# A hybrid encoder block on one core: a new opening, a new end of token mixing, and the gate column stored as single numbers from GpSimd's queue

## The chip, the cores and the metric

The kernel runs on one core of one Trainium2 chip. The metric is device time in microseconds (us). Three runs of the kernel before gave a median of 1852.78 us. One further execution was profiled; every duration below comes from that one.

## The reference, cut to what matters

One layer, one sequence of 256 frames, width 2048, all in float32:

```
mod = silu(c) @ w_ada + b_ada                     # nine vectors of 2048: shift, scale, gate, three times
x  += 1/2 * gt1 * rms(swiglu((rms(x) * (1 + sc1) + sh1) @ w_gu1) @ w_dn1)     # FFN 1, inner width 5504
h   = rms(x) * (1 + sc2) + sh2;  q, k, v, u, w = h @ w_in                     # token mixing
A   = chunked attention(q, k, v) + relative bias;   B = gelu(u) * (W_s norm(gelu(w)) + b)
x  += gt2 * rms(concat(rms(A), rms(B)) @ w_out)
x  += 1/2 * gt3 * rms(swiglu((rms(x) * (1 + sc3) + sh3) @ w_gu2) @ w_dn2)     # FFN 2
```

(The gains of the norms are left out of these lines.) Nothing of this is changed.

## The kernel before, in words

**Matrix products.** Every float32 weight tile is split in two float32r halves: ScalarE casts it (`hi`, L147), VectorE subtracts (`lo = raw - hi`, L148). A product is then three matmuls (L111 to L113): activations hi x weights hi, hi x lo, lo x hi. A weight tile (`raw`, 128 x 2048, 1 MB) arrives by one DMA on SyncE's (SP's) queue into one of three buffers and gives two split pairs of 128 x 1024. The pairs live in slots: four in the pool `wsp`, three more in a stage's own pool (`wx1`, `wx2`, `wx3`). A cast has to wait until the matmuls that read its slot before are done.

**The vectors `mod`.** `w_ada` is stored transposed. `ada_block` (L182) loads 128 rows of it (1 MB) and VectorE multiplies them by the broadcast row `c_bc` and sums along the row: one instruction of 128 x 2048 gives 128 numbers of one vector. There are 144 such blocks. 32 of them (scale and shift of FFN 1) are made in the opening, two for each of the 16 k-tiles (`kt`) of the activations; the other 112 are taken one by one from a list while weights are visited (`tick`), or all that are left of a vector at once (`flush_ada`).

**Opening (L533 to L562, and `first`).** x arrives in two tiles, then the row c as a broadcast of 1 MB, then two small tables. ScalarE squares both x tiles and applies silu to `c_bc`. VectorE scales x by 1/rms, TensorE transposes it, VectorE and ScalarE copy the transposes to `xnT`. `first(kt)` makes the two ada blocks of a k-tile, then `h` on ScalarE (L562), its cast `hhi` (L234) and its rest `hlo` on VectorE (L235). Matmuls on k-tile kt wait for these. To have work for TensorE while few k-tiles are ready, FFN 1 starts with a plan: a *visit* (c, p) takes chunk c of 512 columns and the k-tiles 2p and 2p+1, in 24 matmuls. The plan visits chunks 0, 4, 5, 3, 2, 1 with p = 0, then (1,1), (0,1), (1,2), (0,2), then (2,1) and so on. Chunk 0 keeps its PSUM banks, the others' sums are spilled to SBUF.

**End of token mixing (L866 to L900).** The product with `w_out` goes by two rows of frames (t = 0, 1) and column blocks of 512 (b). The part of B (`m_b`, names `mb`) is done in two pairs of column blocks, each over eight k-tiles and four weight tiles. A pair fills four PSUM banks out of six. When the first pair is done, `evac_b` adds each bank to `y` on VectorE (L867), ScalarE squares it for the norm, and VectorE multiplies by the row `gate` (L267). The second pair does t = 0 over all eight k-tiles, then t = 1. As soon as t = 0 is done, its norm, the addition to x (`post`, L278), the next norm and the transposes of `pre` (L247, `xtp`) lead to FFN 2.

**The gate row** (`gate`, L212 to L226) needs one vector of `mod` (128 partitions x 16 numbers, `gcol`) as a row on all partitions. TensorE transposes the column (`gps`), ScalarE copies it (`grow`), SP stores 16 rows of 512 B to DRAM (`gd`) and loads them back as a broadcast of 1 MB. It is made three times; the one for token mixing is `gate(1, ...)` at the end of mixing.

**Order.** The instructions of each engine stand in an order that a scheduler sets at build time; each engine and each DMA queue works in its order. `after(a, b)` forces a behind b on one engine.

Of the kernel before, what the change touches and what calls it, by code (L numbers as in the profile page):

```python
# [18 lines left out]
P = 128  # L19
# [24 lines left out]
class Lazy:  # L44
# [15 lines left out]
def block_kernel(ctx: ExitStack, tc: tile.TileContext, a: dict, out: bass.AP):  # L60
# [29 lines left out]

    x = load_x(a["x"])
    c_bc = const.tile([P, D], F32, tag="c_bc", name="c_bc")
    nc.sync.dma_start(c_bc, a["c"].partition_broadcast(P))
    vec = const.tile([P, V_N], F32, tag="vec", name="vec")
    nc.sync.dma_start(vec, a["vec"])
    bada = const.tile([P, 9 * KT], F32, tag="bada", name="bada")
    nc.sync.dma_start(bada, a["b_ada"])
# [29 lines left out]

    slots = {"seq": itertools.repeat(wsp), "hold": None}
# [15 lines left out]
    def split(raw):  # L144
# [3 lines left out]
        i_lo = nc.vector.tensor_tensor(lo[:, :n], raw, hi[:, :n].bitcast(F32), op=ALU.subtract)  # L148
        if order["split"]:
# [25 lines left out]
    def ada_block(m, kt, spare=None):  # L175
        if spare:
            st = yp.tile([P, D], F32, tag=spare, name=nm("ada"))
        else:
            st = adap.tile([P, D], F32, tag="ada", name=nm("ada"))
        i = m * KT + kt  # L180
        nc.sync.dma_start(st, a["w_ada"][i * P:(i + 1) * P, :])
        inst = nc.vector.tensor_tensor_reduce(  # L182
# [29 lines left out]
    def gate(i, factor, gp):  # L212
# [13 lines left out]
        nc.sync.dma_start(g, gd[:, :].rearrange("k p -> (k p)").partition_broadcast(P))  # L226
# [35 lines left out]
    def y_done(t, n, y, ysq, g, junk):  # L262

        ns = slice(n * CH, (n + 1) * CH)
        square(junk, y[t][:, ns], ysq[t], n, D)
# [22 lines left out]
    def ffn(wgu, wdn, h, avp, ahp, plan, rate, gate_of, finish, lead=(), after_lead=(), ahead=None):  # L288
# [169 lines left out]
        if plan:  # L458

            kts, credit = 0, 0.0  # L460
            held = plan[0][0]
            first(0)
            raw = gu_load(*plan[0])
            kts = 1
            for v, (c, p) in enumerate(plan):
                while kts < 2 * p + 2:
                    first(kts)
                    kts += 1
                fresh = c not in ps_of
                if fresh:  # L470
# [3 lines left out]
                rest = plan[v + 1:]  # L474
                nxt = [d for d, _ in rest if d != held]
                stop = c not in [d for d, _ in rest] or (c != held and nxt and nxt[0] != c)
                visit(c, p, fresh, bool(stop), bank_outer=v > 0, raw=raw)
                raw = None
                credit += 0.2
                while credit >= 1.0:  # L480
# [524 lines left out]
```

## Time and profile before

| What | us |
|---|---|
| runs, median of 3 | 1852.78 |
| the profiled execution | 1853.2 |
| its span, first to last instruction | 1851.4 |
| TensorE (PE) busy in the span | 1804.0 |
| VectorE (DVE) busy | 1334.6 |
| ScalarE (ACT) busy | 855.0 |
| GpSimd (POOL) busy | 27.6 |

The span leaves 1.8 us around it. PE counts as busy while a matmul is in flight, so time at half clock counts as busy too; the column PEclk of the stage view tells the two apart. In the timeline a row is: start, duration, engine, line, operation, output and input, count, and in brackets how long the engine had been idle and on what.

### The profile page before, as it was taken

The page shows a single profiled execution, that of the slowest core. Times are in us where ns is not written, and L with a number is a line of the kernel's source. Part 1 is how long each engine was busy: PE and PEld are TensorE (multiplying, and loading weights), DVE is VectorE, ACT ScalarE, POOL GpSimd, SP SyncE. Part 2 cuts the span into 40 slices and gives each one's busy share as a digit, 9 for nine tenths or more (in the row PEclk, how much of TensorE's full clock was granted, in tenths as well). Part 3 has the DMA queues.
Part 4 walks back from the last instruction along what each step waited for, and adds up shares of the span by engine and source line. Part 5 has one row for each costly group of instructions (what it writes and reads, how often), then busy time and mean ns, then how long its engine had stood idle before and what let it go on. Part 6 is the DMA issues. An engine that isn't in the chain of part 4 may idle for free.

```text
span 1851.4 us, 21252 instructions
## 1 busy us (share of the span) xinstructions
PE 1804.0 (97%) x8255; PEld 1499.9 (81%) x8255; DVE 1334.6 (72%) x1483; ACT 855.0 (46%) x1095; POOL 27.6 (1%) x54
## 2 busy tenths in 40 slices
PE   5999999999999999999999989999999999999997
PEld 4788888888888898788888867888888888888896
DVE  6888997998878776767889967777445555455455
ACT  5544455454344344745555447444444443443442
POOL 0000000000000000000001000000000000000000
PEclk8999999999999999999999999999999999999999
DMA  8888888889888876478788884887555555555462
GB/s 342 341 317 333 329 329 333 334 338 359 306 335 322 313 276 223 168 288 348 290 318 340 306 320 162 311 331 298 193 184 201 184 187 200 183 195 190 159 245 74
DMA packets 71478, 500.15 MB, mean 270 GB/s; under 512 B 8097, under 2 KB 8273, under 8 KB 12753
## 3 DMA queue, kind: packets, MB, share of 16 engines
q1 hardware_dynamic: 71376, 498.79, 71.2%
q8 instruction: 65, 1.06, 0.2%
q14 instruction: 37, 0.30, 0.0%
HBM read 494.54 MB, written 4.22 MB: 269 GB/s over the span
## 4 chain that ended last, share of the span: by engine, by line
PE 91%; DVE 4%; issue 2%; ACT 2%; DMA 1%; POOL 0%; POOLq 0%; DVEq 0%; ACTq 0%
PE gu L112 16%; PE gu L113 16%; PE gu L111 16%; PE dn L111 8%; PE dn L112 8%; PE dn L113 8%; PE pj L112 4%; PE pj L111 4%; PE pj L113 4%; DVE lo L148 1%; DVE ada L182 1%; PE atp L381 1%; PE wo L112 1%; PE wo L113 1%; PE wo L111 1%
## 5 line engine op out<-in xcount | busy, mean ns | idle before, releaser
L148 DVE TENSOR_TENSOR lo<-raw,hi 128x1024 fp32r<-128x1024 f32 (+1 forms) x628 | 752.0, 1209 | 418.9 <-ACT hi L147 417.5
L147 ACT CAST hi<-raw 128x1024 fp32r<-128x1024 f32 (+1 forms) x628 | 648.6, 1042 | 830.2 <-PE gu L113 453.0
L111 PE MATMUL gu<-hi,hhi 128*128 128x512 f32 (+1 forms) x1396 | 539.0, 387 | 14.8 <-ACT hi L147 7.5
L112 PE MATMUL gu<-lo,hhi 128*128 128x512 f32 (+1 forms) x1396 | 538.4, 386 | 0.1
L113 PE MATMUL gu<-hi,hlo 128*128 128x512 f32 (+1 forms) x1396 | 538.0, 386 | 0.0
L182 DVE CUSTOM_DVE_ANT_0 ada<-ada,c_bc,bada 128x2048 f32<-128x2048 f32 x144 | 337.5, 2345 | 14.6 <-DMA ada<-in_w_ada_dram 14.6
L111 PEld LDWEIGHTS gu<-hi,hhi 128*128 128x128 f32 x1396 | 263.3, 189 | 65.7 <-ACT hi L147 8.2
L112 PEld LDWEIGHTS gu<-lo,hhi 128*128 128x128 f32 x1396 | 263.2, 189 | 50.7 <-DVE lo L148 1.7
L113 PEld LDWEIGHTS gu<-hi,hlo 128*128 128x128 f32 x1396 | 263.2, 189 | 49.8 <-DVE hlo L235 0.2
L111 PE MATMUL dn<-hi,ah 128*128 128x512 f32 x640 | 249.1, 389 | 0.0
L113 PE MATMUL dn<-hi,al 128*128 128x512 f32 x640 | 249.0, 389 | 0.0
L112 PE MATMUL dn<-lo,ah 128*128 128x512 f32 x640 | 249.0, 389 | 0.0
L111 PEld LDWEIGHTS dn<-hi,ah 128*128 128x128 f32 x640 | 120.2, 188 | 25.1
L113 PEld LDWEIGHTS dn<-hi,al 128*128 128x128 f32 x640 | 120.2, 188 | 24.9
L112 PEld LDWEIGHTS dn<-lo,ah 128*128 128x128 f32 x640 | 120.2, 188 | 24.9
L112 PE MATMUL pj<-lo,hhi 128*128 128x512 f32 x304 | 120.9, 398 | 0.0
L111 PE MATMUL pj<-hi,hhi 128*128 128x512 f32 x304 | 120.8, 398 | 0.0
L113 PE MATMUL pj<-hi,hlo 128*128 128x512 f32 x304 | 119.9, 395 | 0.0
L111 PEld LDWEIGHTS pj<-hi,hhi 128*128 128x128 f32 x304 | 57.4, 189 | 11.0
L112 PEld LDWEIGHTS pj<-lo,hhi 128*128 128x128 f32 x304 | 57.3, 189 | 10.9 <-DVE lo L148 0.5
L113 PEld LDWEIGHTS pj<-hi,hlo 128*128 128x128 f32 x304 | 57.1, 188 | 10.9
L416 DVE TENSOR_TENSOR y<-y,dn 128x512 f32<-128x512 f32 x64 | 41.5, 681 | 4.6 <-PE dn L113 4.6
(159 smaller groups left out, 1064.5 us busy)
## 6 DMA issues: line engine op xcount, KB each, us to landing
raw<-in_w_gu_dram SPq DMA_DIRECT2D x160, 1024.0 KB, 4.8
ada<-in_w_ada_dram SPq DMA_DIRECT2D x144, 1024.0 KB, 6.9
raw<-in_w_dn_dram SPq DMA_DIRECT2D x86, 1024.0 KB, 4.8
raw<-in_w_in_dram SPq DMA_DIRECT2D x40, 1024.0 KB, 5.9
raw<-in_w_out_dram SPq DMA_DIRECT2D x16, 1024.0 KB, 7.8
raw<-in_w_gu_dram SPq DMA_DIRECT2D x16, 768.0 KB, 4.4
x<-in_x_dram SPq DMA_DIRECT2D x4, 1024.0 KB, 6.9
x<-x SPq DMA_DIRECT2D x4, 1024.0 KB, 4.7
```

The lines of the kernel that those rows point to most:

```text
L111: nc.tensor.matmul(ps, ah, wh, start=start, stop=False)
L112: nc.tensor.matmul(ps, ah, wl, start=False, stop=False)
L113: nc.tensor.matmul(ps, al, wh, start=False, stop=stop)
L147: i_hi = nc.scalar.copy(hi[:, :n], raw)
L148: i_lo = nc.vector.tensor_tensor(lo[:, :n], raw, hi[:, :n].bitcast(F32), op=ALU.subtract)
L182: inst = nc.vector.tensor_tensor_reduce(out=st, in0=st, in1=c_bc, scale=1.0, scalar=bada[:, i:i + 1], op0=ALU.mult, op1=ALU.add, accum_out ...
L381: nc.tensor.transpose(ps[:, q, :], av[:, q * P:(q + 1) * P], ident)
L416: nc.vector.tensor_tensor(y[t][:, ns], y[t][:, ns], ps[t], op=ALU.add)
```

## The change

1. **c and the tables.** c, `b_ada` and `vec` come as one table `small` (128 x 280) ahead of x. silu is applied to the 16 columns of c; TensorE spreads each over 128 columns (16 transposes of a broadcast column) and VectorE and ScalarE copy four banks to `c_bc`. The load of 1 MB and the silu over 128 x 2048 are gone.
2. **x.** VectorE squares half of the first x tile. The second tile is scaled on ScalarE; all eight copies to `xnT` are on ScalarE, three of them later.
3. **Loads.** The first two ada blocks are loaded right behind x; three more buffers (`early`) hold ada blocks until the plan ends.
4. **Plan.** The first two visits are cut in halves: k-tile 0 for chunks 0 and 4, then k-tile 1 for both, with weights loaded in halves. The order of this start is chained by hand on ScalarE and VectorE. After that each visit's splits are issued one visit ahead, and the ada blocks come one by one: 1.34 for each visit up to k-tile 5, then 0.7 (before: two at once, 0.4 for each visit).
5. **End of mixing.** The first pair of `m_b` runs with 1.5 ada blocks for each weight tile, and the gate row is made behind it in the program. Then two weight tiles of the second pair are split, and `evac_b` stands behind the last of these splits on both engines; x is loaded back after that.
6. **Gate row, all three times.** No transpose and no copy: `gcol` is stored as 2048 single numbers, and the broadcast load follows, both on GpSimd's queue.

```diff
+    small = const.tile([P, KT + 9 * KT + V_N], F32, tag="small", name="small")
+    nc.sync.dma_start(small, a["small"])
     x = load_x(a["x"])
-    nc.sync.dma_start(c_bc, a["c"].partition_broadcast(P))
...
-        ps = ptr.tile([KT, P], F32, tag="tr", name=nm("gps"))
-        nc.tensor.transpose(ps, col, ident)
-        row = sm.tile([KT, P], F32, tag="xn", name=nm("grow"), bufs=2)
-        nc.scalar.copy(row, ps)
         gd = dr.tile([KT, P], F32, tag=f"gd{i}", name=nm("gd"))
-        nc.sync.dma_start(gd, row)
+        with nc.allow_non_contiguous_dma(reason="2048 numbers"):
+            nc.gpsimd.dma_start(gd[:, :].rearrange("k p -> p k"), col)
         g = gp.tile([P, D], F32, tag="gate", name=nm("gate"))
-        nc.sync.dma_start(g, gd[:, :].rearrange("k p -> (k p)").partition_broadcast(P))
+        nc.gpsimd.dma_start(g, gd[:, :].rearrange("k p -> (k p)").partition_broadcast(P))
...
+            chain(first_act, hi0, h0[0], h0[1], late_evac[0], late_evac[1], late_evac[2], hi1, hi2, h1[0], h1[1], hi3)
+            chain(first_dve, *a0, *b0, lo0, h0[2], lo1, *a1, *b1, lo2, h1[2], lo3)
...
-                credit += 0.2
-                while credit >= 1.0:
-                    credit -= 1.0
-                    if kts < KT:
-                        first(kts)
-                        kts += 1
+                if v >= 3 and steps:
+                    credit += 1.34 if steps[0][0] < 6 else 0.7
+                    if steps[0][1] == 2:
+                        step()
+                    while steps and steps[0][1] < 2 and credit >= 1.0:
+                        credit -= step()
...
+    on_act.append(nc.scalar.activation(c_act, c_col, AF.Silu))
+    for j in range(4):
+        ps = pmm.tile([P, 4, P], F32, tag="mm", name=nm("cps"))
+        for q in range(4):
+            nc.tensor.transpose(ps[:, q, :], c_act[:, 4 * j + q:4 * j + q + 1].to_broadcast([P, P]), ident)
...
+        use_slots((wsp, 4), (wx2, 3))
+        tick_acc[1] = 1.5
+        ps = out_pair(m_b)
         flush_ada(GT[1])
         tick_acc[1] = 0.0
         gain(2, 0, KT)
         g = gate(1, 1.0, gp)
-        use_slots((wsp, 4), (wx2, 3))
-        ps = out_pair(m_b)
-        x2.extend(load_x(x_dram))
+        use_slots((adap, 1), once=((wsp, 3), (wx2, 3), (wsp, 1)))
+        sp = wo_visit() + wo_visit()
         for t in range(NT):
             for b in range(2):
-                evac_b(t, b, ps[b][t])
+                evac_b(t, b, ps[b][t], order["last"])
+        x2.extend(load_x(x_dram))
```

**How it moves instructions.** In the rows below ISA with the output `ada` is an ada block and ISA with the output `mod` reads out its sum.

VectorE in the opening, before, from the last part of x to the first split:

```order
L540 TENSOR_SCALAR xn_170<-x_2_89,r_154 128x512
L540 TENSOR_SCALAR xn_177<-x_2_89,r_154 128x512
L555 COPY xnT_185<-xtp_140 128x4x128
L555 COPY xnT_185<-xtp_147 128x4x128
L182 ISA ada_203,mod<-ada_203,c_bc,bada 128x2048
L182 ISA mod 128x1
L193 SCALAR_TENSOR_TENSOR gmul<-mod,vec 128x1
L182 ISA ada_206,mod<-ada_206,c_bc,bada 128x2048
L182 ISA mod 128x1
L235 TENSOR_TENSOR hlo_110<-h_33_210,hhi_109 128x256
L148 TENSOR_TENSOR lo_232<-raw_214,hi_231 128x1024
L148 TENSOR_TENSOR lo_236<-raw_214,hi_235 128x1024
```

and now:

```order
L643 TENSOR_SCALAR xn_174<-x_1_90,r_151 128x512
L643 TENSOR_SCALAR xn_181<-x_1_90,r_151 128x512
L176 TENSOR_REDUCE ms_156<-xsq_153 128x1
L202 ISA ada_114,mod<-ada_114,c_bc,small 128x2048
L202 ISA mod 128x1
L202 ISA ada_116,mod<-ada_116,c_bc,small 128x2048
L202 ISA mod 128x1
L214 SCALAR_TENSOR_TENSOR gmul<-mod,small 128x1
L156 TENSOR_TENSOR lo_240<-raw_226,hi_239 128x1024
L253 TENSOR_TENSOR hlo_113<-h_42_243,hhi_112 128x256
L156 TENSOR_TENSOR lo_248<-raw_228,hi_247 128x1024
L202 ISA ada_230,mod<-ada_230,c_bc,small 128x2048
```

The four scalings of the second x tile and all copies to `xnT` have left VectorE; one half tile of chunk 0 and one of chunk 4 are split before the blocks of k-tile 1.

VectorE at the end of mixing, before, from the last ada block of the gate to the first evacuations (`wo_82..` are the banks of the first pair):

```order
L182 ISA ada_8274,mod<-ada_8274,c_bc,bada 128x2048
L182 ISA mod 128x1
L215 SCALAR_TENSOR_TENSOR gcol_8278<-mod,vec 128x16
L148 TENSOR_TENSOR lo_8363<-raw_8360,hi_8362 128x1024
L148 TENSOR_TENSOR lo_8367<-raw_8360,hi_8366 128x1024
L148 TENSOR_TENSOR lo_8397<-raw_8394,hi_8396 128x1024
L148 TENSOR_TENSOR lo_8401<-raw_8394,hi_8400 128x1024
L867 SCALAR_TENSOR_TENSOR y_1527_7854<-wo_8288,r_8130,y_1527_7854 128x512
L867 SCALAR_TENSOR_TENSOR y_1527_7854<-wo_8290,r_8130,y_1527_7854 128x512
L867 SCALAR_TENSOR_TENSOR y_1528_7855<-wo_8289,r_8137,y_1528_7855 128x512
```

and now (the next row is the first product with `gate`):

```order
L236 SCALAR_TENSOR_TENSOR gcol_8445<-mod,small 128x16
L156 TENSOR_TENSOR lo_8413<-raw_8407,hi_8412 128x1024
L156 TENSOR_TENSOR lo_8417<-raw_8407,hi_8416 128x1024
L202 ISA ada_8409,mod<-ada_8409,c_bc,small 128x2048
L202 ISA mod 128x1
L156 TENSOR_TENSOR lo_8454<-raw_8451,hi_8453 128x1024
L156 TENSOR_TENSOR lo_8458<-raw_8451,hi_8457 128x1024
L156 TENSOR_TENSOR lo_8464<-raw_8461,hi_8463 128x1024
L156 TENSOR_TENSOR lo_8468<-raw_8461,hi_8467 128x1024
L968 SCALAR_TENSOR_TENSOR y_1528_7878<-wo_8286,r_8154,y_1528_7878 128x512
L968 SCALAR_TENSOR_TENSOR y_1528_7878<-wo_8288,r_8154,y_1528_7878 128x512
L968 SCALAR_TENSOR_TENSOR y_1529_7879<-wo_8287,r_8161,y_1529_7879 128x512
```

Four splits of the second pair and one ada block of the next vector now stand ahead of the evacuation.

TensorE in the second pair, before, where the last k-tiles of t = 0 (`wo_8448`, `wo_8450`) give way to t = 1 (`wo_8449`, `wo_8451`) on the first k-tile:

```order
L113 MATMUL wo_8448<-adas_8524,mb_7456 128x512
L111 MATMUL wo_8450<-adas_8524,mb_7455 128x512
L112 MATMUL wo_8450<-adas_8524,mb_7455 128x512
L113 MATMUL wo_8450<-adas_8524,mb_7456 128x512
L113 MATMUL wo_8449<-hi_8454,mb_7456 128x512
L111 MATMUL wo_8451<-hi_8454,mb_7455 128x512
```

and now, where t = 1 (`wo_8492`, `wo_8494`) begins behind the fourth k-tile of t = 0 (`wo_8491`, `wo_8493`, weights `hi_8467`):

```order
L114 MATMUL wo_8493<-lo_8468,mb_7479 128x512
L115 MATMUL wo_8493<-hi_8467,mb_7480 128x512
L113 MATMUL wo_8492<-hi_8453,mb_7479 128x512
L114 MATMUL wo_8492<-lo_8454,mb_7479 128x512
L115 MATMUL wo_8492<-hi_8453,mb_7480 128x512
L113 MATMUL wo_8494<-hi_8453,mb_7479 128x512
```

The first four k-tiles are now done for both t (48 matmuls) before the fifth k-tile of either; t = 0 is complete only 77 matmuls into the pair (before: 50).

More of the change, by code (lines that the diff above doesn't have):

```diff
@@ L126, in after, with chain @@
             mybir.DependencyClass.NoSync, mybir.DependencyReason.DATA), reason="order")
+    def chain(*insts):
+        for first, inst in zip(insts, insts[1:]):
+            after(inst, first)
+        return insts[-1]
     slots = {"seq": itertools.repeat(wsp), "hold": None}
@@ L260, in pre, with y_done @@
         order["ada"] = (inst[1], 2)
[L262 removed]
+    def y_done(t, n, y, ysq, g, junk, behind=None):
         ns = slice(n * CH, (n + 1) * CH)
[L265 removed]
+        inst = square(junk, y[t][:, ns], ysq[t], n, D)
+        if behind:
+            after(inst, behind[0])
         r = rstd(ysq[t]) if n == 3 else None
@@ L458, in ffn @@
         if plan:
-            kts, credit = 0, 0.0
             held = plan[0][0]
[L462 to L466, printed above, removed]
-                    first(kts)
-                    kts += 1
+            other = plan[1][0]
+            lead = [(c, p, (q,)) for q in range(2) for c, p in plan[:2]]
+            halves, late = {}, []
+            for c, p, (q,) in lead:
+                if c not in halves:
+                    halves[c] = wraw.tile([P, 2048], F32, tag="raw", name=nm("raw"))
+                off = 2 * D * CHUNKS[c][0] + p * P * 2048
+                nc.sync.dma_start(halves[c][:, q * 1024:(q + 1) * 1024],
+                                  wgu[off:off + P * 2048].rearrange("(p n) -> p n", p=P)[:, q * 1024:(q + 1) * 1024])
+                if (c, q) == (other, 0):
+                    late = [ada_load(m, 1) for m in (SC[0], SH[0])]
@@ new lines, in ffn, with half @@
+            plan = lead + [(c, p, (0, 1)) for c, p in plan[2:]]
+            ready_sp, dve, acts = {}, [first_dve], [first_act]
+            def half(c, q):
+                ready_sp[c, q] = {q: split(halves[c][:, q * 1024:(q + 1) * 1024])}
+                return order["last"]
+            a0, b0 = ada_first(0, 0, start_ada[0]), ada_first(0, 1, start_ada[1])
+            hi0, lo0 = half(held, 0)
+            h0 = h_first(0)
+            hi1, lo1 = half(other, 0)
+            a1, b1 = ada_first(1, 0, late[0]), ada_first(1, 1, late[1])
@@ L526, in ffn, with end_early @@
         down_last(C - 1, g)
-    h = new_h()
-    pts = []
-    xsq = [new_sums("xsq", 1) for _ in range(NT)]
-    for t in range(NT):
-        junk = yp.tile([P, D], F32, tag="y0", name=nm("junk"))
-        square(junk, x[t], xsq[t], 0, D)
-    nc.scalar.activation(c_bc, c_bc, AF.Silu)
+    wx = ExitStack()
+    wx1 = slots["hold"] = wx.enter_context(tc.tile_pool(name="wx1", bufs=3))
+    es = ExitStack()
+    early["pool"] = es.enter_context(tc.tile_pool(name="early", bufs=3))
+    def end_early():
+        if early["pool"] is not None:
+            early["pool"] = None
+            es.close()
@@ L561, in first, with ada_first, h_first @@
+    late_evac = [i_evac[1, j] for j in range(1, 4)]
+    first_dve = chain(*on_dve)
+    def ada_first(kt, i, st=None):
+        inst = ada_block((SC[0], SH[0])[i], kt, st)
+        return (inst, gain(0, kt, kt + 1)) if i else (inst,)
+    def h_first(kt):
         h32 = sm.tile([P, S], F32, tag="h32", name=nm("h32"), bufs=2)
-        nc.scalar.activation(h32, xnT[kt // 8][:, kt % 8, :], AF.Identity,
-                             bias=mod[:, SH[0] * KT + kt:SH[0] * KT + kt + 1], scale=gmul[:, kt:kt + 1])
```

161 lines of the change are left out of this document (103 added, 58 removed).

## The prediction

> **What bounds the kernel now.** I read the stage view first (stages chosen where the map of 40 slices shows PE below 9; columns: window, length, busy time of PE, PE's weight loads, DVE, ACT, POOL, granted clock, DMA share, GB/s).
>
> ```profile
> span 1851.4 us, 21252 instructions
> 0.00:23.00 23.00, 6.25 (x33) 5.11 (x33) 11.69 (x21) 11.58 (x15) 2.20 (x19) 0.94 0.93 377
> 23.00:52.00 29.00, 25.98 (x98) 20.48 (x99) 21.92 (x22) 17.38 (x25) 0.00 (x0) 0.87 0.76 303
> 52.00:100.00 48.00, 43.63 (x182) 34.60 (x181) 39.14 (x41) 23.52 (x33) 0.00 (x0) 0.96 0.86 339
> 100.00:720.00 620.00, 620.00 (x2822) 519.62 (x2821) 518.88 (x531) 271.73 (x301) 0.00 (x0) 1.00 0.84 322
> 1062.00:1079.00 17.00, 14.67 (x62) 10.58 (x60) 12.04 (x12) 7.89 (x11) 0.00 (x0) 1.00 0.83 322
> 1079.00:1110.00 31.00, 26.52 (x104) 20.91 (x105) 20.42 (x23) 14.85 (x24) 0.00 (x0) 0.89 0.85 335
> 1110.00:1150.00 40.00, 38.03 (x198) 31.68 (x197) 33.10 (x49) 31.32 (x65) 3.90 (x6) 1.00 0.43 158
> ```
>
> PE is the bound: from 100 to 720 it is never idle at full clock. Only its gaps can be won. The opening holds 24.1 us of them up to 100, plus stretches at a lower clock; the end of mixing holds 2.3 + 4.5 + 2.0 us between 1062 and 1150. The change touches both. What ends PE's waits there (us in total, times, longest):
>
> ```profile
> PE gu L111 <- ACT hhi L234: 7.2, 2, 4.3
> PE wo L111 <- ACT hi L147: 5.3, 3, 4.4
> ```
>
> **The opening.** The timeline shows the chain behind these waits.
>
> ```profile
> 8.12 1.91 ACT L162 ACTIVATE junk<-x 128x2048 f32<-128x2048 f32 x1 [0.55 <-DMA x<-in_x_dram]
> 16.03 2.34 DVE L182 CUSTOM_DVE_ANT_0 ada<-ada,c_bc,bada 128x2048 f32<-128x2048 f32 x1
> 20.94 0.60 ACT L562 ACTIVATE h<-xnT,mod,gmul 128x256 f32<-128x256 f32 x1 [4.72 <-DVE mod L182]
> 9.04 6.46 PE L546 MATMUL xtp<-ident,xn 128*128 128x128 f32 x32 [9.04 <-DVE xn L540]
> 22.98 0.80 PE L111 MATMUL gu<-hi,hhi 128*128 128x512 f32 x1 [7.47 <-ACT hi L147]
> 31.17 0.79 PE L111 MATMUL gu<-hi,hhi 128*128 128x512 f32 x1 [2.98 <-ACT hhi L234]
> 80.88 0.43 DVE L235 TENSOR_TENSOR hlo<-h,hhi 128x256 fp32r<-128x256 f32 x1 [1.10 <-ACT hhi L234]
> 80.89 0.50 PE L111 MATMUL gu<-hi,hhi 128*128 128x512 f32 x1 [4.25 <-ACT hhi L234]
> 83.67 0.63 PE L113 MATMUL gu<-hi,hlo 128*128 128x512 f32 x1
> 84.09 0.63 PE L111 MATMUL gu<-hi,hhi 128*128 128x512 f32 x1
> 92.83 0.40 PE L111 MATMUL gu<-hi,hhi 128*128 128x512 f32 x1
> 96.93 0.39 PE L111 MATMUL gu<-hi,hhi 128*128 128x512 f32 x1
> ```
>
> The first ada block starts at 16.03, because VectorE prepares x until then; k-tile 0 is ready at 22.98, k-tile 1 at 31.17, k-tile 5 only at 80.9. Then visit (2,1) ends at 97.2, and nothing waits after that. A matmul costs 0.228 us (18 starts from 92.83 to 96.93), and 0.43 us after a gap, while the clock is low.
>
> The costs of one instruction on VectorE and ScalarE, from the groups of the page (busy, mean ns), and small ones from the timeline:
>
> ```profile
> L148 DVE TENSOR_TENSOR lo<-raw,hi 128x1024 fp32r<-128x1024 f32 (+1 forms) x628 | 752.0, 1209 | 418.9 <-ACT hi L147 417.5
> L147 ACT CAST hi<-raw 128x1024 fp32r<-128x1024 f32 (+1 forms) x628 | 648.6, 1042 | 830.2 <-PE gu L113 453.0
> L182 DVE CUSTOM_DVE_ANT_0 ada<-ada,c_bc,bada 128x2048 f32<-128x2048 f32 x144 | 337.5, 2345 | 14.6 <-DMA ada<-in_w_ada_dram 14.6
> 13.87 1.07 ACT L553 COPY xnT<-xtp 128x512 f32<-128x512 f32 x2 [1.34 <-DVE xnT L555]
> ```
>
> *Start.* The x tiles still come as the first large loads, so the second square can follow its landing at 8.1. Ahead of it ScalarE now has silu of 16 columns, two copies of `c_bc` and half a square; the 16 transposes (before, 32 `xtp` with their waits took 6.5 us) can't start before `small` lands. No row shows `small`; a landing between 2.5 and 5 us bounds it by one x tile's 5, and I take 3.3. Copies then end near 7.6, the half square at 8.8, the second square at 10.9. VectorE's own part is done by then, so its first block starts near 12, not 16.03; two blocks of 2.42 with read-out, and the gain: 17.0, not 20.9. ScalarE has from 12.5 on four scalings and five copies (9 x 0.54 = 4.9), the cast 1.0, h 0.6, `hhi` 0.4: first matmul at 19.4, a lead of 3.6. The old load of c and its silu were not what came last.
>
> *To k-tile 5.* By the new order VectorE does from 12.0 on: 12 ada blocks (29.1), 18 splits (21.1 at 1.17), 6 `hlo` (2.6), 6 gains (1.0), together 53.8. Its waits in the new order: for the first cast behind the copies 1.4; for the second, behind the three late copies, 2.0; for the casts behind `hhi` 0.6; twice for slots that come free only at the end of a visit (1.5 and 1.3), 6.8 in all. Sum 72.6 for `hlo` of k-tile 5, against 81.3. Before, the same work took 65.3 from 16.03, so 11.5 us were waits and copies. At 72.6 PE is just short of work: visits 1 to 8 are 192 matmuls, from 19.4 some 44 us of matmuls with 5 us of low clock and gaps of 2 near k-tile 1, that is about 70; then 20 matmuls of (1,2) and two visits: 68 x 0.228 = 15.5, end of (2,1) at 88.1. **Gain 9.1 us.** Bounds: were VectorE never to wait, 16; were only the start to remain and `small` to land at 5, 2. The DMA cover is thinner than it looks (share 0.93 up to 23), but c's megabyte pays for the earlier ada loads. If the one-ahead splits didn't hide the ada blocks, every block in front of a split would cost 2.4.
>
> **The end of mixing.** Rows of the second place:
>
> ```profile
> 1055.73 2.35 DVE L182 CUSTOM_DVE_ANT_0 ada<-ada,c_bc,bada 128x2048 f32<-128x2048 f32 x1
> 1075.77 0.17 DVE L215 SCALAR_TENSOR_TENSOR gcol<-mod,vec 128x16 f32<-128x16 f32 x1
> 1078.48 0.32 SPq L226 DMA_DIRECT2D gate<-gd  x1
> 1087.25 2.11 DVE L867 SCALAR_TENSOR_TENSOR y<-wo,r,y 128x512 f32<-128x512 f32 x3 [4.99 <-PE wo L113]
> 1089.28 1.89 DVE L267 TENSOR_TENSOR y<-y,gate 128x512 f32<-128x512 f32 x3
> 1093.61 6.90 DVE L148 TENSOR_TENSOR lo<-raw,hi 128x1024 fp32r<-128x1024 f32 x6 [0.24 <-ACT hi L147]
> 1063.46 0.39 PE L111 MATMUL wo<-hi,mb 128*128 128x512 f32 x1
> 1088.79 0.39 PE L113 MATMUL wo<-hi,mb 128*128 128x512 f32 x1
> 1093.63 1.22 PE L111 MATMUL wo<-hi,mb 128*128 128x512 f32 x2 [4.45 <-ACT hi L147]
> 1107.38 1.43 DVE L867 SCALAR_TENSOR_TENSOR y<-wo,r,y 128x512 f32<-128x512 f32 x2 [3.12 <-PE wo L113]
> 1118.65 2.05 PE L247 MATMUL xtp<-dg,x 128*128 128x128 f32 x16 [0.88 <-DVE dg L243]
> ```
>
> *First pair.* 96 matmuls need 21.9 us, so from 1063.46 it could end at 1085.3; it ended at 1089.0. The new order spreads the ada blocks, and I find no wait left: 3.7 us earlier. *Restart.* The second pair needs a bank that `evac_b` frees, and that now stands behind every split. From 1055.73: 12 splits 14.0, 6 blocks 14.5, `gcol` 0.2, and waits of about 4 (for a cast behind ScalarE's four scalings of y, and for weight tiles queued on SP behind ada loads whose buffer is not yet free): 1088.4, plus one evacuation 0.7: PE restarts at 1089.1, before at 1093.63. 4.5 us ahead.
>
> *Given back.* t = 0 is complete after 77 matmuls, not 50. Before, from 1093.63 to 1107.4 was 13.8 for 50 (11.4 and 2.4 of low clock); now 17.5 + 2.4 after 1089.1 is 1109.0. The chain from there (evacuation, gate, norm, x, square, norm) took 11.3 to the first `xtp`; with two evacuations of t = 1 now inside it in place of a split, 11.5. So `xtp` starts at 1120.5 against 1118.65, with 3 matmuls fewer behind it (0.7). PE waits there some 7 us, not 0.9: the lead is lost to this stall. **Loss 1.2**, and 1.3 more for packets of the new stores between the weight loads (bounded by 0 and the 8 us below): 2.5. The bounds are -3 (if t = 0 isn't the last) and +10.
>
> *The gate row.* Its rows (DMA issues, KB each, us to landing; the queue's packets, MB, share):
>
> ```profile
> gate<-gd SPq DMA_DIRECT2D x1, 1024.0 KB, 7.9
> gd<-grow SPq DMA_DIRECT2D x1, 8.0 KB, 1.7
> q1 hardware_dynamic: 71376, 498.79, 71.2%
> ```
>
> Before, `gcol` at 1075.77 led to a landing at 1078.48 + 7.9 = 1086.4, ahead of its use at 1089.28. Now `gcol` comes at 1077.5. From the start of the gate products to the next finished split took 5.5 us (1089.28 to 1093.61 + 1.2), and the order gives PE 48 matmuls that need none of it: until 1089.1 + 10.9 + 2.4 = 1102.4. So the row must land by 1096.9; with 1 us of issue and 7.9 for the broadcast, the store has 10.5 us. No row shows 2048 packets of 4 B. From below, 16 packets took 1.7. From above, each of the 128 packets of an engine waits its turn behind a mean packet of the weights (0.712 x 16 x 1851.4 / 71376 = 0.296 us): 37.8. Ends so far apart are split by their geometric mean, 8: hidden, by 2.5 us. GpSimd waits in its queue between store and load; behind that stands only the norm of t = 0, which comes later. The transpose and copy taken off PE and ACT save 0.5 us of cover. The other two gate rows are made long before use.
>
> **Sum.** 1853.2 (the profiled execution, 0.4 above the median) - 9.1 + 2.5 = **1846.6 us**.
>
> **Rivals.**
> *A, the gate row comes late (slower).* Every microsecond of the store over 10.5 holds VectorE at the first gate product, with the splits of the fifth k-tile behind it, and PE runs dry. At 37.8 the row lands at 1077.5 + 1 + 37.8 + 7.9 = 1124.2, PE stalls 1124.2 - 1096.9 = 27.3: 1873.9, slower than before. It outweighs the gain from a store of 17 us on. For it: the DMA share of 0.85 there, and a share that the queue of weights always fills. Against: PE's stall stops the weight loads, and then the store runs free. Chance 0.2.
> [...]
> *B, the opening is no better.* ScalarE's part per visit in the first round is two casts, four spill copies and h, near 5.2 (2.0 + 4 x 0.54 + 1.0) of the 5.5 us of 24 matmuls; if casts come late by 1 us a visit, the 6.8 of waits become 14 and k-tile 5 arrives at 80: 1853.2 - 2 + 2.5 = 1853.7. Against: ACT is busy for 17.4 of 29 us there now. Chance 0.15.
> *C, both places gain.* A store as cheap as 1.7 and no traffic cost, and an opening with half the waits: 1853.2 - 12.5 - 2 = 1838.7. For it: 24 us of gaps; against: the longer way to t = 0. Chance 0.15.
> The forecast has 0.5.
>
> **How the numbers follow.** The forecast's own range is 1841 to 1852. C lowers the range to 1838, A with a store between 10 and 25 us raises it to 1861: 1838 to 1861 leaves out the far part of A and a little of C. A difference of 2% is about what a measurement of this kernel can tell from no change; it is 37 us, and no case but the far end of A with a further loss reaches it: faster 0.02, same 0.96, slower 0.02.
>
> **What would show it.** First `gu` matmul near 19.4; `hlo` of k-tile 5 near 72.6, (2,1) done near 88. If PE waits more than 5 us between 30 and 88, B. In mixing the first pair ends about 22 us after its start, the restart comes about 4 us later, and PE's longest wait there is in front of `xtp` behind `dg`. If instead the wait stands in front of `hi` or `lo` of the fifth k-tile with VectorE waiting for `gate`, A. The sum is wrong if (2,1) ends within 3 us of 97, or `xtp` comes more than 5 us off.

## The result and the profile after

The changed kernel takes 1865.78 us (median of 4 runs, 1863.36 to 1867.05), the kernel before 1853.28 beside it (median of 4). The ratio is 1.0067, with a 95% interval of 1.0047 to 1.0087: 0.7% slower. One of the four executions of the kernel before took 2025.89 us, and the ratio leaves it out. The profiled execution of the changed kernel has a span of 1862.8 us, 11.4 more than before.

The stage view of the changed kernel, in the stages of the prediction:

```profile
span 1862.8 us, 21298 instructions
0.00:23.00 23.00, 11.91 (x50) 9.93 (x50) 10.75 (x17) 13.54 (x23) 4.22 (x19) 1.00 0.92 363
23.00:52.00 29.00, 26.92 (x106) 21.55 (x105) 25.04 (x26) 18.27 (x28) 0.00 (x0) 0.94 0.84 351
52.00:100.00 48.00, 46.96 (x205) 37.59 (x204) 42.77 (x48) 26.14 (x35) 0.00 (x0) 1.00 0.97 390
100.00:720.00 620.00, 613.30 (x2772) 510.93 (x2771) 509.08 (x520) 266.04 (x294) 1.91 (x2) 1.00 0.82 313
1062.00:1079.00 17.00, 17.00 (x77) 14.08 (x76) 14.82 (x14) 7.68 (x9) 0.00 (x0) 1.00 0.85 335
1079.00:1110.00 31.00, 23.95 (x95) 17.96 (x93) 16.45 (x18) 8.30 (x13) 1.77 (x2) 0.94 1.00 288
1110.00:1150.00 40.00, 31.80 (x158) 27.05 (x159) 34.86 (x52) 33.20 (x69) 4.75 (x6) 0.91 0.51 189
```

Up to 100 us PE's gaps have shrunk: it is busy for 85.8 us there, not 75.9. But between 100 and 720, where before nothing waited, PE now stands still for 6.7 us, and between 1079 and 1150 for 15.2, not 6.5.

A table of stages with fixed bounds doesn't tell where the time went once everything has shifted. So I also numbered PE's wide matmuls (128x512, and 128x384 for the last chunk of `gu`) of the outputs `gu`, `dn`, `pj` and `wo` in the order of their starts (7632 in either trace) and compared the start of the k-th one. Minus is a lead over the kernel before:

| k | start before, us | place | changed kernel, us |
|---|---|---|---|
| 0 | 22.98 | first `gu` | -0.6 |
| 264 | 96.93 | end of visit (2,1) | -7.7 |
| 700 | 195.76 | first round | -4.3 |
| 1000 | 265.87 | end of the first round | -1.5 |
| 1400 | 358.36 | ahead of the hole at the first gate (below) | -1.5 |
| 1600 | 404.59 | behind it | +4.0 |
| 4300 | 1064.37 | first pair of `m_b` | +4.1 |
| 4400 | 1097.62 | second pair, just restarted | +0.2 |
| 4500 | 1126.94 | behind the `xtp` of t = 0 | +11.9 |
| 7000 | 1704.90 | second FFN | +11.4 |

Four things happened. The opening won 7.7 us; the first round took 6.2 of it back; 5.5 were lost near the first gate, a place to which the prediction gave nothing; and at the end of mixing 3.9 were won and 11.7 lost. The third gate (near 1285) cost nothing.

What ended PE's waits in the changed kernel:

```profile
PE wo L113 <- ACT hi L155: 8.0, 3, 4.7
PE xtp L265 <- DVE dg L261: 6.5, 1, 6.5
PE gu L113 <- ACT hhi L252: 4.2, 2, 2.2
PE gu L113 <- DVE acc L376: 4.2, 6, 1.1
PE dn L114 <- DVE lo L156: 1.8, 1, 1.8
```

`acc` is the spill of the first round: those six waits lie between 90 and 245 us. The wait in `dn` begins at 371.7, behind the first gate; behind it PE's granted clock is 0.51 from 373.8 to 377.3, where before it is 1.00.

The DMA view from 350 to 370 us, first of the changed kernel (GB/s in slices of 0.5 us; the other rows are the queue, the number of issues, KB each and the median us from issue to landing):

```profile
GB/s 426 426 426 328 393 311 410 492 229 229 344 344 410 377 393 344 377 378 334 319 100 0 49 82 82 66 66 49 66 82 33 66 33 49 66 33 131 66 393 410
ada<-in_w_ada_dram SPq DMA_DIRECT2D x2, 1024.0 KB, 16.3
raw<-in_w_gu_dram SPq DMA_DIRECT2D x2, 1024.0 KB, 13.6
gd<-gcol POOLq DMA_DIRECT2D x1, 8.0 KB, 13.3
```

and of the kernel before, which makes no transfer for the gate there:

```profile
GB/s 442 410 410 311 377 311 377 377 180 213 98 213 442 311 442 360 410 492 344 442 344 279 147 295 459 426 360 492 393 410 475 393 410 262 311 360 442 344 229 33
```

The store is issued at 353.5 and lands 13.3 us later; from 360 to 369 (18 slices) the whole core's transfers fall to some 60 GB/s. Weights under way then take 14 to 16 us from issue to landing; over the program their medians are 4.8 and 6.9. A second hole, of some 80 GB/s for 10 us, stands at the end of mixing; in the changed kernel from 1080 to 1100:

```profile
GB/s 377 361 229 246 360 360 360 279 377 393 410 459 393 414 301 233 49 33 99 49 33 83 246 49 180 147 164 66 33 49 33 33 16 49 82 131 197 393 377 410
q1 hardware_dynamic: 587, 4.27, 98.8%
x<-x SPq DMA_DIRECT2D x2, 1024.0 KB, 24.3
raw<-in_w_out_dram SPq DMA_DIRECT2D x2, 1024.0 KB, 20.2
gate<-gd POOLq DMA_DIRECT2D x1, 1024.0 KB, 10.3
gd<-gcol POOLq DMA_DIRECT2D x1, 8.0 KB, 14.0
```

Two weight tiles of `w_out` landed after 20 us, and VectorE shows what that did (timeline of the changed kernel):

```profile
1081.32 0.17 DVE L236 SCALAR_TENSOR_TENSOR gcol<-mod,small 128x16 f32<-128x16 f32 x1
1094.11 2.36 DVE L156 TENSOR_TENSOR lo<-raw,hi 128x1024 fp32r<-128x1024 f32 x2 [6.37 <-ACT hi L155]
1100.35 2.36 DVE L156 TENSOR_TENSOR lo<-raw,hi 128x1024 fp32r<-128x1024 f32 x2 [3.88 <-ACT hi L155]
1102.63 2.06 DVE L968 SCALAR_TENSOR_TENSOR y<-wo,r,y 128x512 f32<-128x512 f32 x3
1107.13 1.90 DVE L287 TENSOR_TENSOR y<-y,gate 128x512 f32<-128x512 f32 x3 [2.44 <-DMA gate<-gd]
```

The wait for the gate row itself is only 2.4 us. Ten more were already lost in front of the splits, behind casts whose weights came late. ScalarE's waits between 1062 and 1145 say whose they were:

```profile
ACT hi L155 <- DMA raw<-in_w_out_dram: 23.0, 4, 9.5
```

Before, the same group in this place was 5.6 us.

### The profile page after: what moved, and what is told of

Its sections match the earlier page's. It is cut to its first block, busy times and chain, and to the rows that moved or that the text cites. A ratio compares the mean times of both kernels' runs of the same rounds, so it can differ in the third digit from the quotient of the medians.

```text
span 1862.8 us, 21298 instructions
## 1 busy us (share of the span) xinstructions
PE 1810.7 (97%) x8268; PEld 1503.7 (81%) x8268; DVE 1331.7 (71%) x1479; ACT 856.4 (46%) x1102; POOL 36.5 (2%) x60
## 5 line engine op out<-in xcount | busy, mean ns | idle before, releaser
L202 DVE CUSTOM_DVE_ANT_0 ada<-ada,c_bc,small 128x2048 f32<-128x2048 f32 x144 | 337.3, 2344 | 24.2 <-DMA ada<-in_w_ada_dram 15.3
L178 POOL TENSOR_TENSOR r<-ms,mhalf 128x1 f32<-128x1 f32 x16 | 21.8, 1361 | 1033.5 <-DVE ms L176 1033.5
```

The costliest lines, as they stand in the source:

```text
L178: nc.gpsimd.tensor_tensor(r, ms, mhalf, op=ALU.pow)
L202: inst = nc.vector.tensor_tensor_reduce(out=st, in0=st, in1=c_bc, scale=1.0, scalar=bada[:, i:i + 1], op0=ALU.mult, op1=ALU.add, accum_out ...
```

## The experiments

Theory T1 was that the 2048 pieces of 4 bytes starve the weights wherever they are stored. T2 put it down to GpSimd's queue, T3 to the rebuilt order, with a store that costs nothing. Each run below changes the changed kernel, unless it says otherwise; "lead" is that of the table above, against the same trace of before. "Span" is that of the one profiled execution. Executions of one kernel differ by up to 6 us, so a difference of 1 or 2 us between two spans says little by itself.

**1. The old gate path back in the changed kernel.**

```diff
+        ps = ptr.tile([KT, P], F32, tag="tr", name=nm("gps"))
+        nc.tensor.transpose(ps, col, ident)
+        row = sm.tile([KT, P], F32, tag="xn", name=nm("grow"), bufs=2)
+        nc.scalar.copy(row, ps)
...
-        with nc.allow_non_contiguous_dma(reason="2048 numbers"):
-            nc.gpsimd.dma_start(gd[:, :].rearrange("k p -> p k"), col)
+        nc.sync.dma_start(gd, row)
...
-        nc.gpsimd.dma_start(g, gd[:, :].rearrange("k p -> (k p)").partition_broadcast(P))
+        nc.sync.dma_start(g, gd[:, :].rearrange("k p -> (k p)").partition_broadcast(P))
```

> The change with the gate path of before at all three places: transpose on TensorE, copy on ScalarE, store of 16 rows of 512 B and broadcast load on SyncE's queue. Theory T1 (the store of 2048 single numbers keeps the DMA engines from the weights for about 9 us wherever it stands): the lag against before stays at -1.5 us through the first gate (in the changed kernel it goes there from -1.5 to +4.0), and at the end of mixing ScalarE's waits for w_out weights fall from 23 us to under 10; span 1848 to 1852 (the changed kernel 1862.8). T3 (the new order at the end of mixing and the lead spent between 95 and 240 us are all of it, the store costs nothing): span within 3 us of 1862.8.

Span 1851.1, median 1851.85; ratio to before 0.9995 (0.9985 to 1.0005). The lead is 9.5 at k = 264 and 3.4 at k = 1000, and stays at 3.5 from k = 1400 to 1600; ScalarE's waits for `w_out` are 9.3 us. T1 holds and T3 falls. But the kernel is no faster than before either: with the store gone, the rest of the change shows no gain as a whole. A caveat: the transpose is put in PE's order at 687 us, so the first gate's transfers also stand elsewhere now; run 5 closes that.

**2. Rows of 512 B, but on GpSimd's queue** (`nc.gpsimd` in place of `nc.sync` for the store and the load of run 1).

> As the run with the row gate, but store (16 rows of 512 B) and broadcast load are issued by GpSimd. T1 (packet size): store lands in under 5 us, span within 2 us of the run with the row gate on SyncE's queue. T2 (it is GpSimd's queue, not the size of the packets): store and load still take 10 us or more each, span 1858 or more.

Span 1850.3 (one execution), store 3.7 us in the median. T2 falls: with rows the queue alone costs nothing (run 1 has 1851.1).

**3. Single numbers, but on ScalarE's queue** (`nc.scalar.dma_start(gd...)`).

> The change with only the store of 2048 single numbers moved from GpSimd's queue to ScalarE's; the broadcast load stays on GpSimd's. T1: the store still takes 9 us or more and the weights' rate falls under 100 GB/s for that time; span 1858 or more. T2: store in under 5 us, span 1848 to 1853.

```profile
gd<-gcol ACTq DMA_DIRECT2D x3, 8.0 KB, 17.9
q10 hardware_dynamic: 6192, 0.02, 0.2%
```

Span 1867.3 (one execution), at least as slow as from GpSimd. Here the trace counts each piece: 6192 packets are three times 2064. T2 falls again, but T1 holds in part only. At the first gate the rate does fall under 100 GB/s, for some 5 us, and 5.2 us of lead go. At the end of mixing it does not. The store is issued at 1079.6 and takes 24.9 us; these are the rates from 1080 to 1120 (slices of 1 us) and PE's wait there:

```profile
GB/s 311 410 418 426 402 393 434 426 443 402 393 418 443 434 410 377 402 451 369 183 42 9 0 0 0 0 213 393 401 41 0 8 0 0 0 0 0 0 139 385
PE wo L113 <- ACT hi L155: 15.2, 1, 15.2
```

Up to 1098 the transfers run at 311 to 451 GB/s beside the store. Here the row itself is late: VectorE waits 16.2 us for it, with the fifth k-tile's splits behind. So the same 2048 pieces cost time in two ways, and which one prevails differs with the queue and the place.

**4. Only the new gate path, in the kernel before.**

> The kernel before with only the gate path of the change (2048 single numbers and the broadcast load on GpSimd's queue). T1: lag of 3 to 6 us at the first gate (near 375 to 400 us), and 5 to 12 us more at the end of mixing, where the gate row would land 14 + 1 + 10 us behind its column (1075.8), near 1101, against its use at 1089: span 1860 to 1870 (before 1851.4). T3: within 3 us of 1851.4.

Span 1865.5, in the shortest of four executions; median 1871.22, ratio 1.0101 (1.0084 to 1.0118). The lag is +6.2 behind the first gate and +14.3 behind mixing. At the end of mixing VectorE shows

```profile
DVE y L264 <- DMA gate<-gd: 12.7, 1, 12.7
```

so in the old order, which has nothing to do meanwhile, the row itself is waited for. The span lies inside T1's range; the price at the first gate is just over its 3 to 6 us, that in mixing (8.1) inside.

**5. The column as it lies in SBUF: 128 pieces of 64 B, same queue, same place.**

```diff
-        gd = dr.tile([KT, P], F32, tag=f"gd{i}", name=nm("gd"))
-        with nc.allow_non_contiguous_dma(reason="2048 numbers"):
-            nc.gpsimd.dma_start(gd[:, :].rearrange("k p -> p k"), col)
+        gd = dr.tile([P, KT], F32, tag=f"gd{i}", name=nm("gd"))
+        nc.gpsimd.dma_start(gd, col)
...
-        nc.gpsimd.dma_start(g, gd[:, :].rearrange("k p -> (k p)").partition_broadcast(P))
+        nc.gpsimd.dma_start(g, gd[:, :].rearrange("p k -> (p k)").partition_broadcast(P))
```

> The change with the gate column stored as it lies in SBUF, 128 pieces of 64 B that follow one another in DRAM, on GpSimd's queue; the broadcast load reads the 8 KB as before, so the gate values come in another order than the reference's: the output is not the reference's, only the time counts. Theory N (the number of pieces is what costs, 2048 against 128): the store lands in under 5 us, no stretch of 9 us with the weights under 100 GB/s, span 1848 to 1853 as with the rows. Rival (any write of pieces under 512 B costs it): store 10 us or more, span 1858 or more.

Stores 5.2 us in the median, a little over the forecast's 5; span 1849.2. ScalarE still waits 15.2 us for `w_out` at the end of mixing, but PE only 1.7 for `hi`, so ScalarE's waits alone don't measure the price. From 352 to 372 us, around the first store at 353.6, the rates are

```profile
GB/s 229 311 410 410 410 328 262 344 262 442 377 395 417 398 395 492 295 213 344 98 229 393 393 442 393 344 442 426 410 410 426 459 410 442 426 442 410 393 442 442
```

and the lead goes through the first gate unchanged (-1.4 at k = 1400 and 1600). This run has the same opening as the changed kernel (-7.6 at k = 264), so the difference of their spans, 1862.8 - 1849.2 = 13.6 us, is the price of cutting the store into 4 bytes (one execution each). So the rival falls: here 128 pieces of 64 B cost little, 2048 of 4 B those 13.6 us. The edit changes the number of the pieces, their size and their distance in DRAM (512 B from one to the next, now none) together; no run separates the three.

That leaves the other half: why does the change without the store win nothing?

**6. Fewer ada blocks in the first round** (run 1, `else 0.7` to `else 0.4`).

> The change with the row gate, and the pace of ada blocks behind k-tile 5 set back from 0.7 to 0.4 a visit (the pace of before). Theory P (in the first round the change lets VectorE do about nine ada blocks, 22 us of work, more by 240 us than before did, so the spills come late and PE waits: that eats 5.9 us of the 9.8 us lead): the lead at the thousandth big matmul (266 us) is 8 us or more instead of 3.9, and the span 1844 to 1847. Theory O (the blocks are harmless; the spills are late because the next visit's splits now stand ahead of them): as without it, lead 3.9, span 1850 to 1852.

Slower: span 1865.5, ratio 1.0077 (1.0060 to 1.0094). The 9.5 us of lead become a lag of 13.8:

```profile
PE gu L113 <- ACT hhi L255: 16.5, 7, 5.7
```

Theory P falls in this form: the blocks were needed, and PE now waits for k-tiles, with 2.1 us of waits for spills beside them.

**7. Spills ahead of the next splits** (run 1, `prep(v + 1)` moved behind the spills).

> The change with the row gate, and in the first round the next visit's splits issued behind the spills instead of ahead of them. Theory O: lead at the thousandth big matmul 8 us or more, span 1844 to 1847. Theory P: lead 3 to 5 us, span 1850 to 1852.

Lead 4.4, span 1849.1, ratio 0.9992 (0.9983 to 1.0001), and PE still waits 4.0 us for spills. Theory O falls.

**8. Half of VectorE's time for ada blocks from k-tile 6 on** (scale and shift of FFN 1 only; run 9's kernel with `st[:, :wd]`, `wd = D // 2`).

> The opening of the change with the row gate and the end of mixing of before, and the ada blocks of the first vector from k-tile 6 on take the product over 1024 of their 2048 columns (half of VectorE's time for them; that part of the sums is left out, so the output is not the reference's). Theory S (VectorE's work in the first round is all that the time there holds): the lead at the thousandth big matmul is 8 us or more instead of 3.9, and PE's waits for spills fall from 4.2 us to under 1. Rival (ScalarE's casts or the slots of the split weights set the pace there): lead 3 to 5 us.

The waits for spills fall to 0.8 us, as theory S says:

```profile
PE gu L113 <- DVE acc L380: 0.8, 3, 0.3
100.00:340.00 240.00, 239.15 (x1066) 196.78 (x1065) 196.26 (x235) 109.21 (x129) 0.00 (x0) 1.00 0.83 320
```

The lead at k = 1000 is 5.8, between the two forecasts; but it began from 7.8 at k = 264 and not from 9.8. From there to k = 1000 it gives back 2.0 us, where run 9, the same kernel without this edit, gives back 6.2; the changed kernel, which begins from 7.7, gives back 6.2 too. So two thirds of that loss are VectorE's work; the last 2 us stay open.

**9. The opening alone, with the end of mixing of before** (and the row gate).

> The opening of the change with the row gate and with the end of mixing of before. If the rebuilt end of mixing costs what the lags of the run with the row gate say (a lead that goes from 2.6 to 11 us and back to 1.2): span 1846.5 to 1849, the lead of 3.9 staying to the end. Rival (the rebuilt end gains, and the opening's lead would be lost in mixing anyway): span 1851 or more.

Span 1848.0, median 1850.65, ratio 0.9986 (0.9977 to 0.9995). The lead of 3.5 at k = 1000 stays to the end, at 3.3. In run 1 the lead goes from 2.2 at k = 4300 over 10.6 at most to 0.3 (the forecast has 2.6, 11 and 1.2), here from 2.9 to 3.3. So by the two traces the rebuilt end of mixing costs 2.3 us even without its store; the medians, 1850.65 and 1851.85, differ by 1.2.

**10. t = 0 before t = 1 in the second pair** (run 1, and the first matmul of t = 1 forced behind the last of t = 0).

> The change with the row gate, and in the second pair of m_b all matmuls of t = 0 forced ahead of those of t = 1 (complete after 50 or fewer matmuls of the pair, not 77). Theory (PE's wait of 6.5 us for dg ahead of xtp comes from t = 0 being complete late): that wait falls under 3 us, xtp starts 3 to 6 us earlier, span 1845 to 1849. Rival (the weights of the last k-tiles are late whatever the order): the wait moves in front of their hi or lo, span 1850 to 1853.

```profile
PE wo L113 <- ACT hi L155: 7.1, 3, 3.5
PE xtp L268 <- DVE dg L264: 1.0, 1, 1.0
```

Span 1850.1, ratio 0.9995 (0.9986 to 1.0004). The wait of 6.5 us in front of `xtp` is gone and 7.1 us stand in front of the weights' `hi`. The span is the rival's. Its reason, late weights, is what run 11 tests.

**11. The same with rows on GpSimd's queue.**

> Rows of 512 B on GpSimd's queue (SyncE's queue no longer stands behind the copy of the row) together with t = 0 ahead of t = 1 in the second pair. Theory W (in the run with t = 0 first PE waited 7.1 us for weights of w_out, because their loads stood in SyncE's queue behind the store of the row): that wait falls to 3 us or less, the lead behind the wait for dg is 4 us or more instead of 1.2, span 1845 to 1848. Rival (the weights are late for their bytes or their buffers, not for the queue): span 1849 to 1851.

PE's wait there is 8.9 us, not 3 or less; span 1851.1, ratio 0.9991 (0.9981 to 1.0001). Theory W falls. ScalarE waits only 3.6 us for `w_out`, so it isn't the loads either; VectorE's timeline shows the place:

```profile
1094.90 1.90 DVE L290 TENSOR_TENSOR y<-y,gate 128x512 f32<-128x512 f32 x3 [3.63 <-DMA gate<-gd]
1099.24 3.50 DVE L156 TENSOR_TENSOR lo<-raw,hi 128x1024 fp32r<-128x1024 f32 x3 [0.24 <-ACT hi L155]
```

Four evacuations from 1089.2 on, the wait for the gate row and the gate products stand ahead of the last splits, and PE runs dry behind them.

**12. The gate products behind the last splits** (run 11, and:)

```diff
-        nc.vector.tensor_tensor(y[t][:, ns], y[t][:, ns], g[:, ns], op=ALU.mult)
+        if not defer:
+            nc.vector.tensor_tensor(y[t][:, ns], y[t][:, ns], g[:, ns], op=ALU.mult)
...
+        for t in range(NT):
+            for b in range(2):
+                ns = slice(b * CH, (b + 1) * CH)
+                after(nc.vector.tensor_tensor(y[t][:, ns], y[t][:, ns], g[:, ns], op=ALU.mult), order["last"][1])
```

> Rows on GpSimd's queue, t = 0 first, and the four products of the first pair with the gate row put behind the splits of the last k-tiles on VectorE (they are needed only when y is added to x). Theory V (VectorE's chain of evacuations, gate wait and products ahead of the last splits sets when t = 0 is complete, not the weights' loads): PE's wait for the last k-tiles' hi falls from 8.9 us to 4 or less, xtp starts 4 to 6 us earlier (by the clock of before at 1112 to 1115), span 1845 to 1848. Rival (weights late in SyncE's queue): wait and span as without it, 1850 to 1852.

```profile
PE wo L113 <- ACT hi L155: 4.4, 2, 3.1
1112.12 2.05 PE L268 MATMUL xtp<-dg,x 128*128 128x128 f32 x16 [0.43 <-DVE dg L264]
```

`xtp` starts at 1112.1, where run 11 has 1118.2; less the 1.5 us by which run 12 was ahead at k = 4300, that is 4.6 earlier. PE's wait in front of `hi` falls by half, to 4.4 us, a little over the forecast's 4. Span 1846.0, median 1848.29, ratio 0.9976 (0.9966 to 0.9986). Theory V holds.

**13. Pace and order of the first round, on run 11** (spills ahead of the next splits as in run 7, and `else 0.7 if steps[0][0] < 10 else 0.58`).

> As the run with rows on GpSimd's queue and t = 0 first, and in the first round the spills ahead of the next splits and ada blocks at 0.7 a visit up to k-tile 9 and 0.58 behind it. If a part of VectorE's early blocks is only too early (theory P in a weaker form): lead at the thousandth big matmul 5.5 to 8 us, span 1.5 to 4 us under the run without it. If VectorE's work in the first round is simply as much as the time there holds (theory S): lead 3 to 5 us, PE waiting for hhi or for spills, span within 1.5 us of it.

Span 1849.4, median 1851.63, ratio 0.9993 (0.9983 to 1.0002). From k = 264 to 1000 it gives back 5.0 us, run 11 gives back 6.2: 1.2 us won. PE still waits 3.1 us for spills, as theory S says. The lead at k = 1000 is 2.7, under the 3 to 5 of the forecast, since either run entered the first round with 7.6 or 7.7 and not 9.8 (the clock, in the last section). The spans differ by 1.7, a little more than S allows, the medians (1851.63, run 11 1851.45) not at all.

**14. All that helped, joined** (run 12 with that pace and order).

> All that helped so far in one kernel: the gate products behind the last splits, t = 0 first, rows on GpSimd's queue, and in the first round spills ahead of the next splits with ada blocks at 0.7 a visit up to k-tile 9 and 0.58 behind it. If the two places add up: 1 to 2 us under the run with the gate products behind, 1844 to 1847. If what the first round wins is lost in mixing to the same chain on VectorE: equal to it within 1 us.

Median 1847.62, ratio 0.9972 (0.9961 to 0.9984), span 1846.1. It is under both kernels, 0.3% under before. The lead at k = 1000 is 4.8 us, in run 12 it is 3.4; behind mixing they are 5.3 and 5.4. The two places don't add up: what the first round keeps is lost again in mixing.

## Why the prediction was wrong

**The opening's gain, right at its place.** Predicted was `hlo` of k-tile 5 at 72.6 and the end of (2,1) at 88.1. The changed kernel's rows:

```profile
12.53 2.34 DVE L202 CUSTOM_DVE_ANT_0 ada<-ada,c_bc,small 128x2048 f32<-128x2048 f32 x1
22.41 1.22 PE L113 MATMUL gu<-hi,hhi 128*128 128x512 f32 x2 [2.15 <-ACT hhi L252]
31.75 0.50 PE L113 MATMUL gu<-hi,hhi 128*128 128x512 f32 x1 [2.08 <-ACT hhi L252]
73.58 0.42 DVE L253 TENSOR_TENSOR hlo<-h,hhi 128x256 fp32r<-128x256 f32 x1
```

VectorE starts its blocks at 12.5 (predicted 12.0) and `hlo` of k-tile 5 comes at 73.6. The next visit begins at 89.2, a gain of 7.7; in the nine runs whose clock did not drop at 32 us it is 9.5 to 10.0. The term was 9.1. Two errors inside cancel: the first matmul came at 22.4, not 19.4, because ScalarE's four scalings began at 15.3 behind the norm of the second tile; but the two half visits of k-tile 0 carried PE over it. Rival B, the opening no better, falls.

**"Nothing waits after that" is the first step that failed.** The sum carries the gain of the opening to the end and puts a loss in the first round at nothing. The prediction read this from PE's row alone, 620.00 of 620 us busy. The same row had VectorE at 518.9, and in the first round the kernel before shows it (the column after the weight loads') at 90%:

```profile
100.00:340.00 240.00, 240.00 (x1076) 198.76 (x1075) 216.45 (x239) 111.38 (x131) 0.00 (x0) 1.00 0.85 328
```

Of the lead, 6.2 us went back there. 5.2 of them are the six stops in front of spills, counted from start to start of the matmuls (4.2 us of them are waits in the view above). Spills are VectorE's work, and run 8, with less other work for VectorE, loses only 2.0. The 90% don't tell the size by themselves: they leave 23.5 us idle, more than the lead, and yet most of it went.

**The first pair, right; the restart, right by luck.** PE's first and last matmul of the pair and the restart in the changed kernel, and the `xtp` that follows:

```profile
1067.54 0.39 PE L113 MATMUL wo<-hi,mb 128*128 128x512 f32 x1
1089.07 0.39 PE L115 MATMUL wo<-hi,mb 128*128 128x512 f32 x1
1094.13 1.22 PE L113 MATMUL wo<-hi,mb 128*128 128x512 f32 x2 [4.67 <-ACT hi L155]
1129.54 5.79 PE L265 MATMUL xtp<-dg,x 128*128 128x128 f32 x24 [6.52 <-DVE dg L261]
```

The pair takes 21.9 us, with no wait in it. `gcol` came at 1081.3, predicted 1077.5 on a clock that stands 4.1 us earlier there. PE restarts after a stop of 4.7 us, predicted 4. But the prediction had the second pair wait for a bank that `evac_b` frees behind every split. The trace has the first evacuation at 1102.63, 8.5 us *after* the restart: no bank was missing, as a pair fills four of six. What PE waited for was `hi`, a cast whose weights the store held back. Without 4-byte stores there is no such stop: in run 1 the second pair begins at 1085.1, 0.2 us behind the start of the first pair's last matmul, that is 1087.3 by the clock of before (predicted 1089.1). The wrong wait and the store's cost fell on the same number.

**t = 0 and `xtp`, right but for the store.** PE's longest wait is in front of `xtp`, behind `dg`: 6.5 us, predicted some 7. In run 1, without the store, its row is

```profile
1117.98 5.43 PE L268 MATMUL xtp<-dg,x 128*128 128x128 f32 x24 [6.50 <-DVE dg L264]
```

with a lead of 2.2 at k = 4300, that is 1120.1 by the clock of before; predicted was 1120.5. Two errors cancel here too: the second pair began 1.8 us earlier than predicted, and then PE waited 1.9 us in three places for its splits. The loss of 1.2 measured 1.9 there (from 2.2 to 0.3). In the changed kernel `xtp` came at 1129.54, 1125.5 by the clock of before.

**The gate row is the step that cost the sign.** Three parts of it failed. GpSimd's issues in the changed kernel:

```profile
1081.80 1.21 POOL L242 DMA_DIRECT2D gd<-gcol  x1 [29.45 <-DVE gcol L236]
1096.38 0.56 POOL L244 DMA_DIRECT2D gate<-gd  x1 [13.37 <-issue]
```

*The store* was taken as 8 us, between 1.7 and 37.8; it took 14.0. The upper end was the author's estimate, in which each packet waits behind one of the weights; no run shows such turns. The 1 us of issue was an estimate too: the two issues took 1.21 and 0.56. The load behind the store took 10.3 in place of 7.9, so the row landed at 1096.4 + 10.3 = 1106.7, 5.7 us behind the latest time that the prediction allowed for it, 1096.9, which is 1101.0 on this clock. *The packets* were to cost 1.3 us between the weight loads; the loads fell to 60 to 80 GB/s for 9 or 10 us at a time. And *"the other two gate rows are made long before use"* asked when the row is needed, not what its store does to others: the first one cost 5.5 us without anyone waiting for it. The sum of these terms, 1.3, measured 13.6 (run 5 against the changed kernel). Rival A named the right operation, and for the changed kernel the wrong victim: VectorE waited 2.4 us for the row, ScalarE 23.0 for weights. In runs 3 and 4 its victim is the right one (VectorE waits 16.2 and 12.7 us for the row). Its argument against itself, that a stall of PE frees the store, is refuted by the rates: the store was slow while the weights' transfers stood at 60 GB/s.

**The sum.** Without the store the forecast would have been 1853.2 - 9.1 + 1.2 = 1845.3; run 1 measured a span of 1851.1, and with the 1.8 us around it 1852.9. Of the 7.6 us between them 6.1 are the lead lost in the first round, 1.3 more went between k = 1000 and 4300, and 0.7 more than forecast at the end of mixing; the opening won 0.4 more than forecast. In the changed kernel the opening won 7.7 us, 6.2 went in the first round, 5.5 at the first gate, 0.1 up to k = 4300 and 7.3 at the end of mixing: +11.4, where the forecast had -6.6.

## What to carry to other kernels

A transfer is priced by what it does to the transfers beside it, at every place where it is made, not only by when its result is needed (the first gate's store cost 5.5 us here while nobody waited for it): count its pieces, and look at GB/s in the slices behind its issue. A lead won for the busiest engine needn't last to the end (of 7.7 us here 6.2 went in the next stage): look in the stage behind the edit at the engine that is nearly as busy, and at what the busiest one takes from it, before counting the gain to the end. A number that comes out as predicted doesn't show the reason: look whether the wait named is the one in the trace. And where one engine frees a bank, adds a late row and prepares the next weights, put the work whose result is needed last behind the work that feeds the bound.

## What the runs showed of the hardware

**4-byte pieces.** A store of 2048 of them took 12 to 16 us from GpSimd's queue and 14 to 25 from ScalarE's; 128 pieces of 64 B took 5 to 7, 16 rows of 512 B 1.3 to 5. Beside it, in the changed kernel, the weights' own packets grew longer: by the queue's row above, 587 packets in 98.8% of 16 engines and 20 us are 0.54 us each. In run 1, from 1072 to 1092, the row is

```profile
q1 hardware_dynamic: 1002, 7.05, 89.4%
```

which makes 0.29 us. In run 3 the trace counts 2064 packets on the queue of the store from 1080 to 1120, 2.9% of 16 engines in 40 us: 9 ns each. Spread evenly over 16 engines, an estimate from that row, it would be 1.2 us. On GpSimd's queue, in the changed kernel from 1080 to 1100, the trace has only 48 packets for the same store, 0.9% of 16 engines in 20 us. What fills the rest of the store's time, and why the weights' packets lengthen meanwhile, no row here shows.

**PE's clock after a short gap.** All 14 kernels with the new opening have a gap in front of the first `gu` of k-tile 1. In six profiles, the changed kernel's among them, it was 1.98 to 2.15 us, and in five of the six 7 or 8 matmuls ran at 0.43 us in place of 0.228 about a microsecond later (not in run 3, with 2.00); in the other eight it was 0.70 to 1.40 us, and none did. From run 11 and run 12:

```profile
31.82 0.50 PE L113 MATMUL gu<-hi,hhi 128*128 128x512 f32 x1 [2.14 <-ACT hhi L255]
```

```profile
31.48 0.50 PE L113 MATMUL gu<-hi,hhi 128*128 128x512 f32 x1 [1.23 <-ACT hhi L255]
```

Gap and clock together are worth 1.9 us of lead (1.8 against 3.8 at k = 96), and it is why spans of these runs should be compared only between equal openings. In the changed kernel the gap is 29.7 to 31.75, and the granted clock is 0.50 from 32.5 to 35.9. In run 3 the gap is 29.3 to 31.3, and the clock stays at 1.00. So a gap of 2 us went with a lower clock in five profiles of six, and one of 0.70 to 1.40 us in none of eight; what sets run 3 apart, no run here shows.
